# Two transposes moved from a DMA detour to VectorE, and a new way into the kernel: loads of x from ScalarE's queue, zero-tile passes ahead of the data, squares of x from a token-major load

## The chip, the cores and the metric

The kernel runs on one core of one Trainium2 chip. The metric is device time in microseconds, from the start to the end of one execution; the median of three runs is shown. Engines are named as in the profile: PE is TensorE's matmul side, PEld its weight load, DVE is VectorE, ACT is ScalarE, POOL is GpSimd, SP is SyncE, which issues most DMAs.

## What is computed

One residual block with two parallel token mixers, on 256 tokens of width 2048, all in float32:

```
h = RMSNorm(x);  p = h @ W_in
y_m = mlstm(p) @ W_up_m          # 4 heads, chunkwise, width 1024
y_s = s5(p) @ W_up_s             # 32 groups, 64 complex states each, width 512
merged = sigmoid(g_m) * y_m + sigmoid(g_s) * y_s
x = x + merged @ W_out
x = x + SwiGLU(RMSNorm(x))       # hidden width 5632
out = RMSNorm(x)
```

## The kernel before

**Blocks.** All weights are cut into blocks of 128 partitions x 1024 float32 (512 KB): two contraction tiles of 128 rows by 512 columns. The list `blocks` (L1139 to L1165) holds 427 of them in the order of use: `w_in`, the small head matrices, `w_glu`, `w_up_s` (8 blocks), `w_up_m` (16: four column quarters n of four blocks), `w_out` (32: four quarters of eight), the FFN's gate and up matrices and `w_ffn_down`. A float32 product is made of three passes: each operand is split into a rounded part hi and a rest lo, and hi\*hi, hi\*lo and lo\*hi are summed (`o2_block`, L160). `emit_dma` (L136) loads a block into a `raw` buffer from SP's queue, `emit_split` (L147) makes hi on ScalarE (L156) and lo = raw - hi on VectorE (L157). There are three `raw` and three hi/lo buffers; in the FFN every fourth block takes a `raw` from the ten larger `u8` buffers as soon as one is free.

**Order of the work.** The main loop (L1234) goes over the blocks. In iteration i it emits the load of block i+5, the split of block i+2, block i's passes with what follows them, and what earlier blocks left for later. `later(fn, delay)` (L1169) does that: work with delay 1 runs one iteration after the present one, with delay 0 at the end of the present list. `pump` (L208) places pieces of the S5 and mLSTM mixers between blocks during the first 140. A scheduler then orders each engine's instructions; `tc.issue_after` keeps an instruction behind another on its engine.

**The start.** x comes transposed (`xT`, feature-major) in five loads on SP's queue, between the first block loads (L1178, L1227, L1241). `xt_split` (L1184) scales it by the norm's gain and splits it into `hTh` and `hTl`. For the norm itself `xt_square` (L1197) squares the same tiles on ScalarE, pair by pair, and sums them on VectorE; `rms1` (L1206) sums over partitions with eight small passes on TensorE against a tile of ones and makes the reciprocal root `r1`, which is needed at the first evacuation of an accumulator. The first blocks are quarter 4 of `w_in`, whose passes are 256 columns wide (L853).

**The two transposes.** A product's result has tokens on the partitions; the next product needs features there. `upm_mm` (L951) forms a merged tile of 128 tokens x 512 features on VectorE after a quarter's last block and calls `turn` (L969). That transposes 32x32 squares inside their groups of 32 partitions (`blocks_T`, L273, one instruction of 128x512), and one iteration later moves the groups between the partitions by way of DRAM: `groups_dma` (L278) issues one write and four reads on GpSimd's queue. Two iterations after that the tile is split into `mTh` and `mTl`. `out_mm` (L988) adds the product to x after each quarter, and `x1_T` (L1008) does the same for the residual tiles: transposes, move, and a scale-and-split into `h2h` and `h2l`. There are eight merged and eight residual tiles. Contraction tiles 12 to 15 of `mTh`, the last merged quarter, are first read by block 6 of each quarter of `w_out`. The FFN uses `turn` too (22 tiles, L1068).

Of the kernel before, what the change touches and what calls it, by code (L numbers as in the profile page):

```python
# [17 lines left out]
P = 128  # L18
# [23 lines left out]
SQ = 3  # L42
GLU = 3
SLACK = 0.3


@with_exitstack
def block_kernel(ctx: ExitStack, tc: tile.TileContext, d, out):
# [18 lines left out]
    def u8(shape, dt=F32, name="u"):  # L67
        return up.tile(shape, dt, tag="u8", name=nm(name), bufs=NU8)
# [24 lines left out]
    def TT(o, a, b, op):  # L93
        return V.tensor_tensor(o, a, b, op=op)  # L94
# [7 lines left out]
    def f(ap):  # L102
        return ap.bitcast(F32)
# [5 lines left out]
    def pvs(n, i=None, w=1):  # L109
        a, b = PV[n]  # L110
        if i is None:
            return pv[:, a:b]
        return pv[:, a + i : a + i + w]
# [17 lines left out]
                blocks.append((d[name][n, kp], fn_maker, (n, kp)))  # L131

    raws, splits = {}, {}
    wdma = [None]

    def emit_dma(i):  # L136
        if i < len(blocks):
            if i == 3:
                raw = u32([P, 1024], name="raw")
            elif FFN0 + 4 <= i < len(blocks) - NTAIL - 4 and i % 4 == 3:  # L140
                raw = u8([P, 1024], name="raw")
            else:
                raw = wp.tile([P, 1024], F32, tag="raw", name=nm("raw"), bufs=NRAW)
            wdma[0] = nc.sync.dma_start(raw, blocks[i][0]).ins
            raws[i] = raw

    def emit_split(i):  # L147
        if i < len(blocks):
            raw = raws.pop(i)
            if i >= len(blocks) - NTAIL:  # L150
                hl = u8([P, 2, 1024], F32R, name="hl")
                hi, lo = hl[:, 0], hl[:, 1]
            else:
                hi = wp.tile([P, 1024], F32R, tag="hi", name=nm("hi"), bufs=NHI)
                lo = wp.tile([P, 1024], F32R, tag="lo", name=nm("lo"), bufs=NHI)
            A.copy(hi, raw)  # L156
            TT(lo, raw, f(hi), SUB)  # L157
            splits[i] = (hi, lo)

    def o2_block(acc, lhs, kts, hi, lo, first, last):  # L160
# [112 lines left out]
    def blocks_T(o, i):  # L273
        V.transpose(o.rearrange("p j a c -> p a j c"), i.rearrange("p (a j c) -> p a j c", a=4, j=4))  # L274
# [676 lines left out]
    def upm_mm(i, nk, hi, lo):  # L951
        n, kp = nk
        if n == 0 and kp == 0:
            mlg.until("out")
            cur["mTh"] = [u8([P, 8, 256], F32R, name="mTh") for _ in range(2)]
            cur["mTl"] = [u8([P, 8, 256], F32R, name="mTl") for _ in range(2)]
        oh, ol = ml["out"]
        if kp == 0:
            cur["acc"] = [acc_tile(), acc_tile()]
        o2_block(cur["acc"], lhs_of([oh], [ol], 8), (2 * kp, 2 * kp + 1), hi, lo, kp == 0, kp == 3)  # L960
        if kp == 3:
            for tt in range(2):
                o = gate_ap("gm", tt, n)
                TT(o, cur["acc"][tt], o, MUL)
                TT(o, o, gate_ap("gs", tt, n), ADD)
                v = lambda a: a[n // 2][:, n % 2 * 4 : n % 2 * 4 + 4, :]
                turn(n, tt, o, v(cur["mTh"]), v(cur["mTl"]))

    def turn(n, tt, src, th, tl):  # L969
        st_ = m2([P, 4, 4, 32])  # L970
# [35 lines left out]
            later(lambda: x1_T(n))  # L1006

    def x1_T(n):  # L1008
        sd = u8([P, 2, 1024], name="x1sd")
        st_ = sd[:, 0].rearrange("p (t j a c) -> p t j a c", j=4, t=2, a=4)  # L1010
        for tt in range(2):
            blocks_T(st_[:, tt], cur["x1"][:, tt, n * 512 : n * 512 + 512])

        def move():
            for tt in range(2):
                groups_dma(
                    sd[:, 1].rearrange("p (t i x) -> p t i x", t=2, i=4)[:, tt],
                    sd[:, 0].rearrange("p (t j x) -> p t j x", j=4, t=2)[:, tt],
                )
            later(split)  # L1020

        def split():
            d_ = sd[:, 1].rearrange("p (t i a c) -> p a (t i) c", i=4, t=2, a=4)
            for a in range(4):
                ct = 4 * n + a
                v = lambda h: h[ct // 8][:, ct % 8, :].rearrange("p (i c) -> p i c", c=32)
                A.activation(v(cur["h2h"]), d_[:, a], AF.Copy, scale=pvs("g2", ct))
                STT(v(cur["h2l"]), d_[:, a], pvs("g2", ct), f(v(cur["h2h"])), MUL, SUB)

        later(move, 0)  # L1030
        if n == 3:
            s = cp.tile([P, 2], F32, name="ssum2")
            V.tensor_reduce(s, ss2, mybir.AxisListType.X, ADD)
            TS(s, s, 1.0 / D, EPS, MUL, ADD)
            rstd(r2, s, "r2")
# [133 lines left out]
    def later(fn, delay=1):  # L1169
        laters.append([delay, fn])  # L1170
# [1 line left out]

    SL = NHI - 1
    DL = SL + NRAW
    xt = {}
    s1 = cp.tile([P, 2], F32, name="s1")

    def xt_dma(a, n):  # L1178
        t = (u16 if a >= 8 else u8)([P, n, 256], name="xt")
        nc.sync.dma_start(t.rearrange("p a b -> p (a b)"), d["xT"][:, a * 256 : (a + n) * 256])  # L1180
        for k in range(n):
            xt[a + k] = t[:, k, :]

    def xt_split(kp):  # L1184
        for kt in (2 * kp, 2 * kp + 1):
            oh_ = hTh[kt // 8][:, kt % 8, :]
            ol_ = hTl[kt // 8][:, kt % 8, :]
            g = pvs("gmix", kt)
            A.activation(oh_, xt[kt], AF.Copy, scale=g)
            STT(ol_, xt[kt], g, f(oh_), MUL, SUB)  # L1190

    one2 = cp.tile([P, 2], F32, name="one2")
    nc.gpsimd.memset(one2, 1.0)
    A.copy(cp.tile([P, 2], F32, name="warm"), one2)
    xq = u8([P, 3, 512], name="xq")

    def xt_square(kp):  # L1197
        a = xt[2 * kp]
        b = xt[2 * kp + 1]
        o = xq[:, 0 if kp == 0 else 1 + kp % 2]  # L1200
        A.activation(o[:, 0:256], a, AF.Square)
        A.activation(o[:, 256:512], b, AF.Square)
        if kp:
            TT(xq[:, 0], xq[:, 0], o, ADD)

    def rms1():  # L1206
        ps_ = aux()
        for tt in range(2):
            for h in range(2):
                c = h * 256 + tt * 128  # L1210
                mm(ps_[:, tt * 2 : tt * 2 + 2], xq[:, 0, c : c + 128], one2, h == 0, h == 1)
        TS(s1, ps_[:, 0:4].rearrange("p (a b) -> p a b", b=2)[:, :, 0], 1.0 / D, EPS, MUL, ADD)
# [12 lines left out]
    s5g = Gen(s5_gen())  # L1225
    mlg = Gen(ml_gen())
    for k in range(4):  # L1227
        xt_dma(*((0, 2), (2, 2), (4, 4), (8, 4))[k])
        emit_dma(k)
    for kp in range(2):  # L1230
        xt_split(kp)
        emit_split(kp)

    for i in range(len(blocks)):  # L1234
        if i == 0:
            for k in range(4, DL):
                emit_dma(k)
        emit_dma(i + DL)
        with tc.issue_after(wdma[0]):
            if i == 0:  # L1240
                xt_dma(12, 4)  # L1241
# [3 lines left out]
            if i == 4:  # L1245
                nc.sync.dma_start(cst, d["cst"])
                A.copy(identr, ident)
                A.copy(maskr, maskf)
            if i == 9:
                nc.sync.dma_start(wif, d["wif"])  # L1250
            if i == 6:
                s5["bT"] = u8([P, 4, 2, 128], name="s5bT")
                nc.sync.dma_start(s5["bT"], d["s5bT"])
        if i + SL < 8:
            xt_split(i + SL)
        emit_split(i + SL)
        if 0 <= i - SQ + 1 < 8:
            xt_square(i - SQ + 1)
        hi, lo = splits.pop(i)
        blocks[i][1](i, blocks[i][2], hi, lo)  # L1260
        run = [l for l in laters if l[0] <= 0]
        laters = [[l[0] - 1, l[1]] for l in laters if l[0] > 0]
        if i == 6 + SQ:
            rms1()
        for l in run:
            l[1]()
        fn, (n, kp) = blocks[i][1], blocks[i][2]
        t = 2.59 if fn in (win_mm, ups_mm, upm_mm) else 1.31
        if fn is win_mm and kp == 7 and n > 4:
# [85 lines left out]
```

## Time and profile before

| what | value |
|---|---|
| median of 3 runs | 1259.12 us (1258.21 to 1259.77) |
| the profiled execution's own time | 1258.85 us |
| its span in the profile | 1257.1 us |
| PE, PEld busy | 1233.7 us (98%), 1015.3 us |
| DVE, ACT, POOL busy | 803.8 us (64%), 604.0 us (48%), 106.6 us |
| mean granted clock of TensorE | 0.995 |
| DMA on GpSimd's queue (the detours) | 7904 packets, 19.94 MB |
| all DMA | 258.19 MB, mean 205 GB/s |

The span runs from the first to the last instruction; 1.75 us of the execution's own time lie around it. Passes on TensorE overlap: a pass of 512 columns is listed with 0.39 us while passes start some 0.23 us apart, so a busy PE is not a PE at its peak, and counts of passes in windows of equal length say more. The idle time of an engine off the chain costs nothing.

### The profile page before, as it was taken

The page shows a single profiled execution, that of the slowest core. Times are in us where ns is not written, and L with a number is a line of the kernel's source. Part 1 is how long each engine was busy: PE and PEld are TensorE (multiplying, and loading weights), DVE is VectorE, ACT ScalarE, POOL GpSimd, SP SyncE. Part 2 cuts the span into 40 slices and gives each one's busy share as a digit, 9 for nine tenths or more (in the row PEclk, how much of TensorE's full clock was granted, in tenths as well). Part 3 has the DMA queues.
Part 4 walks back from the last instruction along what each step waited for, and adds up shares of the span by engine and source line. Part 5 has one row for each costly group of instructions (what it writes and reads, how often), then busy time and mean ns, then how long its engine had stood idle before and what let it go on. Part 6 is the DMA issues. An engine that isn't in the chain of part 4 may idle for free.

```text
span 1257.1 us, 15683 instructions
## 1 busy us (share of the span) xinstructions
PE 1233.7 (98%) x5738; PEld 1015.3 (81%) x5738; DVE 803.8 (64%) x1162; ACT 604.0 (48%) x752; POOL 106.6 (8%) x199
## 2 busy tenths in 40 slices
PE   7999999999999999989999999999999999999997
PEld 7777888887788878868888888888888888888885
DVE  8779945999877856645556555555555554554544
ACT  7574554446654445444344444434444443444433
POOL 0000000000000522211101100110111010000000
PEclk9999999999999999989999999999999999999999
DMA  7645655554555977877667766555765686666443
GB/s 265 208 137 178 194 184 182 167 160 143 190 182 193 280 265 256 286 239 224 217 203 228 222 212 217 187 184 204 245 228 183 225 279 198 196 198 199 152 161 141
DMA packets 75597, 258.19 MB, mean 205 GB/s; under 512 B 10496, under 2 KB 11264, under 8 KB 75520
## 3 DMA queue, kind: packets, MB, share of 16 engines
q1 hardware_dynamic: 67616, 237.25, 58.1%
q0 software_dynamic: 7904, 19.94, 4.8%
q8 instruction: 45, 0.74, 0.2%
q14 instruction: 32, 0.26, 0.1%
HBM read 245.09 MB, written 12.06 MB: 205 GB/s over the span
## 4 chain that ended last, share of the span: by engine, by line
PE 85%; DVE 6%; DMA 5%; issue 2%; ACT 1%; ACTq 0%; SPq 0%; DVEq 0%
PE acc L100 80%; PE aux L100 4%; DMA raw<-in_w_out_dram 4%; DVE lo L94 3%; ACT hi L156 1%; DMA raw<-in_w_ffn_gate_dram 1%; DVE xcT L97 1%; DVE stm L94 0%; DVE bu L94 0%; DMA raw<-in_w_up_m_dram 0%; DVE x L94 0%; DVE gm L94 0%; DMA raw<-in_w_in_dram 0%; PE aux L774 0%; DVE h2l L97 0%
## 5 line engine op out<-in xcount | busy, mean ns | idle before, releaser
L94 DVE TENSOR_TENSOR lo<-raw,hi 128x1024 fp32r<-128x1024 f32 x427 | 521.0, 1221 | 403.6 <-ACT hi L156 403.0
L156 ACT CAST hi<-raw 128x1024 fp32r<-128x1024 f32 x427 | 449.1, 1053 | 577.5 <-PE acc L100 488.9
L100 PE MATMUL acc<-lo,h2h 128*128 128x512 f32 x704 | 275.2, 391 | 0.6 <-DVE lo L94 0.5
L100 PE MATMUL acc<-hi,h2l 128*128 128x512 f32 x704 | 274.2, 390 | 0.0
L100 PE MATMUL acc<-hi,h2h 128*128 128x512 f32 x704 | 246.8, 391 | 4.2 <-ACT hi L156 4.2
L100 PE MATMUL acc<-hi,aT 128*128 128x512 f32 x664 | 204.6, 389 | 0.0
L100 PEld LDWEIGHTS acc<-hi,h2h 128*128 128x128 f32 x704 | 132.5, 189 | 32.7 <-ACT hi L156 5.3
L100 PEld LDWEIGHTS acc<-lo,h2h 128*128 128x128 f32 x704 | 132.7, 189 | 29.6 <-DVE lo L94 2.1
L100 PE MATMUL acc<-lo,hTh 128*128 128x512 f32 x384 | 153.6, 400 | 1.3 <-DVE lo L94 1.2
L100 PEld LDWEIGHTS acc<-hi,h2l 128*128 128x128 f32 x704 | 132.8, 189 | 27.4
L100 PE MATMUL acc<-hi,hTl 128*128 128x512 f32 x384 | 150.4, 392 | 0.0
L100 PEld LDWEIGHTS acc<-hi,aT 128*128 128x128 f32 x664 | 124.7, 188 | 25.9
L100 PE MATMUL acc<-hi,hTh 128*128 128x512 f32 x384 | 139.4, 393 | 0.0
L100 PE MATMUL acc<-lo,aT 128*128 128x512 f32 x332 | 129.1, 389 | 0.0
L100 PEld LDWEIGHTS acc<-lo,hTh 128*128 128x128 f32 x384 | 72.1, 188 | 22.1 <-DVE lo L94 4.0
L100 PEld LDWEIGHTS acc<-hi,hTh 128*128 128x128 f32 x384 | 71.7, 188 | 16.7 <-issue 2.0
L100 PEld LDWEIGHTS acc<-hi,hTl 128*128 128x128 f32 x384 | 72.2, 188 | 14.6 <-issue 0.7
L281 POOL DMA_DIRECT2D bounce<-m x30 | 16.9, 565 | 690.5 <-DVE m L274 690.2
L100 PEld LDWEIGHTS acc<-lo,aT 128*128 128x128 f32 x332 | 62.3, 188 | 12.9
L283 POOL DMA_DIRECT2D m<-bounce x120 | 65.6, 554 | 43.1 <-DMA bounce<-m 28.2
L100 PE MATMUL acc<-lo,mTh 128*128 128x512 f32 x128 | 50.0, 392 | 0.0
L100 PE MATMUL acc<-hi,mTl 128*128 128x512 f32 x128 | 49.5, 389 | 0.0
(246 smaller groups left out, 1077.7 us busy)
## 6 DMA issues: line engine op xcount, KB each, us to landing
raw<-in_w_in_dram SPq DMA_DIRECT2D x104, 512.0 KB, 3.5
raw<-in_w_ffn_gate_dram SPq DMA_DIRECT2D x88, 512.0 KB, 3.7
raw<-in_w_ffn_up_dram SPq DMA_DIRECT2D x88, 512.0 KB, 4.2
raw<-in_w_ffn_down_dram SPq DMA_DIRECT2D x88, 512.0 KB, 3.5
raw<-in_w_out_dram SPq DMA_DIRECT2D x32, 512.0 KB, 5.0
raw<-in_w_up_m_dram SPq DMA_DIRECT2D x16, 512.0 KB, 3.6
bounce<-m POOLq DMA_DIRECT2D x30, 256.0 KB, 4.1
m<-bounce POOLq DMA_DIRECT2D x120, 64.0 KB, 4.2
```

Source lines behind the costliest of these rows:

```text
L94: return V.tensor_tensor(o, a, b, op=op)
L97: return V.scalar_tensor_tensor(out=o, in0=a, scalar=s, in1=b, op0=op0, op1=op1, **kw)
L100: return PE.matmul(o, l, r, start=start, stop=stop, skip_group_check=True)
L156: A.copy(hi, raw)
L281: nc.gpsimd.dma_start(bounce, st_)
L283: nc.gpsimd.dma_start(dt_[32 * j : 32 * j + 32], bounce.rearrange("(i r) j x -> r i j x", i=4)[:, :, j])
```

## The change

Merged tiles and residual tiles are no longer moved through DRAM. `blocks_across` transposes each 32x32 square straight to its place in another partition group: sixteen VectorE instructions a tile, each from 32 partitions to 32 partitions, four squares (128 columns) wide. The two tiles of a merged quarter are turned at the end of its last block's iteration and one iteration later, those of a residual quarter one and two iterations after its last block; the scale-and-split of the residual then comes in operations of 128 columns instead of 256. The FFN's `turn` stays. At the start, the first eight tiles of `xT` come in four loads on ScalarE's queue, with the activation table's first load behind them; block 0 is loaded, and split, in two halves; six passes on a zeroed tile, which feed nothing, are put ahead of TensorE's work. The squares are taken from a second load of x, token-major, 2 MB on SP's queue at blocks 3 and 4: four ScalarE operations of 1024 columns that sum as they go, emitted at block 8. The constants' load moves from block 4 to 5.

```diff
+NWARM = 6
...
+    def pieces(i):
+        return (slice(0, 512), slice(512, 1024)) if i == 0 else (slice(0, 1024),)
...
-            wdma[0] = nc.sync.dma_start(raw, blocks[i][0]).ins
+            for p_ in pieces(i):
+                wdma[0] = nc.sync.dma_start(raw[:, p_], blocks[i][0][:, p_]).ins
...
-            A.copy(hi, raw)
-            TT(lo, raw, f(hi), SUB)
+            for p_ in pieces(i):
+                last = A.copy(hi[:, p_], raw[:, p_]).ins
+                TT(lo[:, p_], raw[:, p_], f(hi[:, p_]), SUB)
+                if i == 0 and p_.start == 0:
+                    with tc.issue_after(last):
+                        xt_split_kt(1)
...
-                turn(n, tt, o, v(cur["mTh"]), v(cur["mTl"]))
+                later(lambda tt=tt, o=o, th=v(cur["mTh"]), tl=v(cur["mTl"]): turn_here(n, tt, o, th, tl), tt)
+
+    def blocks_across(o, i):
+
+        v = i.rearrange("p (a j c) -> p a j c", a=4, j=4)
+        for q in range(4):
+            for j in range(4):
+                V.transpose(o[32 * j : 32 * j + 32, :, 32 * q : 32 * q + 32], v[32 * q : 32 * q + 32, :, j])
+
+    def turn_here(n, tt, src, th, tl):
+        dt_ = m2([P, 4, 128])
+        blocks_across(dt_, src)
+        v = lambda a: a[:, :, tt * 128 : tt * 128 + 128]
+        A.copy(v(th), dt_)
+        TT(v(tl), dt_, f(v(th)), SUB)
...
     def x1_T(n):
...
+        d_ = u8([P, 4, 256], name="x1d")
+
+        def part(tt):
+            ts_ = slice(tt * 128, tt * 128 + 128)
+            blocks_across(d_[:, :, ts_], cur["x1"][:, tt, n * 512 : n * 512 + 512])
             for a in range(4):
                 ct = 4 * n + a
+                v = lambda h: h[ct // 8][:, ct % 8, ts_]
+                A.activation(v(cur["h2h"]), d_[:, a, ts_], AF.Copy, scale=pvs("g2", ct))
+                STT(v(cur["h2l"]), d_[:, a, ts_], pvs("g2", ct), f(v(cur["h2h"])), MUL, SUB)
+
+        part(0)
+        later(lambda: part(1), 0)
...
+    zw = m2([P, 256])
+    nc.gpsimd.memset(zw, 0.0)
+    zp = aux()
+    for k in range(NWARM):
+        mm(zp[:, 0:256], zw[:, 0:128], zw, True, True)
+    for a, n in ((0, 1), (1, 1), (2, 2), (4, 4)):
+        xt_dma(a, n, nc.scalar)
...
+    with tc.issue_after(adma[0]):
+        A.copy(cp.tile([P, 2], F32, name="warm"), one2)
+    ssx = cp.tile([P, 2, 2], F32, name="ssx")
+
+    def x_squares():
         for tt in range(2):
             for h in range(2):
+                v = xs[0][:, tt, h * 1024 : h * 1024 + 1024]
+                A.activation(v, v, AF.Square, accum_out=ssx[:, tt, h : h + 1])
...
     def rms1():
+        TT(s1, ssx[:, :, 0], ssx[:, :, 1], ADD)
+        TS(s1, s1, 1.0 / D, EPS, MUL, ADD)
         rstd(r1, s1, "r1")
...
-    for k in range(4):
-        xt_dma(*((0, 2), (2, 2), (4, 4), (8, 4))[k])
+    for k in range(3):
         emit_dma(k)
-    for kp in range(2):
-        xt_split(kp)
-        emit_split(kp)
+    xt_dma(8, 4, nc.sync)
+    emit_dma(3)
+    xt_split_kt(0)
+    emit_split(0)
+    xt_split(1)
+    emit_split(1)
...
+            if i == 3:
+                xs.append(u16([P, 2, 2048], name="xs"))
+            if i in (3, 4):
+                nc.sync.dma_start(xs[0][:, i - 3], d["x"][(i - 3) * 128 : (i - 2) * 128])
+            if i == 5:
                 nc.sync.dma_start(cst, d["cst"])
...
-        if 0 <= i - SQ + 1 < 8:
-            xt_square(i - SQ + 1)
+        if i == 8:
+            x_squares()
```

## Rows read from the trace of the kernel before

**Rows 1.** The chain of waits, its shares of the span by engine and line.

```profile
by line: PE acc L100 80.3%; PE aux L100 4.4%; DMA raw<-in_w_out_dram 3.5%; DVE lo L94 2.6%; issue 1.6%; ACT hi L156 1.2%; DMA raw<-in_w_ffn_gate_dram 1.2%; DVE xcT L97 0.7%; DVE stm L94 0.5%; DVE bu L94 0.4%; DMA raw<-in_w_up_m_dram 0.4%; D
```

**Rows 2.** Windows of 4 us: length, busy of PE, PEld, DVE, ACT, POOL, clock, DMA, GB/s.

```profile
20.00:24.00 4.00, 4.00 (x36) 4.00 (x35) 4.00 (x12) 2.75 (x7) 0.00 (x0) 1.00 0.60 160
448.00:452.00 4.00, 2.47 (x10) 1.57 (x10) 2.89 (x3) 1.57 (x2) 0.00 (x0) 1.00 0.79 276
532.00:536.00 4.00, 3.21 (x15) 2.32 (x13) 0.00 (x0) 0.00 (x0) 0.21 (x1) 1.00 1.02 398
536.00:540.00 4.00, 1.68 (x3) 0.96 (x4) 1.72 (x2) 2.62 (x3) 4.00 (x8) 0.72 0.89 337
540.00:544.00 4.00, 4.00 (x10) 2.72 (x9) 1.86 (x2) 0.42 (x1) 0.15 (x1) 0.50 0.83 262
544.00:548.00 4.00, 2.35 (x9) 1.51 (x9) 2.71 (x5) 2.65 (x5) 0.00 (x0) 0.93 0.63 194
552.00:556.00 4.00, 4.00 (x19) 3.32 (x18) 1.97 (x2) 3.84 (x5) 0.00 (x0) 1.00 0.55 157
```

**Rows 3.** Timeline of VectorE in w_up_m: start, us, instruction.

```profile
405.68 1.22 DVE L94 TENSOR_TENSOR lo<-raw,hi 128x1024 fp32r<-128x1024 f32 x1 [1.08 <-ACT hi L156]
408.39 1.22 DVE L94 TENSOR_TENSOR lo<-raw,hi 128x1024 fp32r<-128x1024 f32 x1 [1.50 <-ACT hi L156]
409.54 1.28 DVE L94 TENSOR_TENSOR gm<-acc,gm 128x512 f32<-128x512 f32 x2
410.74 1.28 DVE L94 TENSOR_TENSOR gm<-gm,gs 128x512 f32<-128x512 f32 x2
411.94 1.22 DVE L94 TENSOR_TENSOR lo<-raw,hi 128x1024 fp32r<-128x1024 f32 x1
413.07 1.29 DVE L274 STREAM_TRANSPOSE m<-gm 128x512 f32<-128x512 f32 x2
414.29 1.18 DVE L94 TENSOR_TENSOR lo<-raw,hi 128x1024 fp32r<-128x1024 f32 x1
...
419.09 0.68 DVE L94 TENSOR_TENSOR mTl<-m,mTh 128x512 fp32r<-128x512 f32 x1
```

**Rows 4.** Timeline at the first FFN blocks, idle time before and its releaser in brackets.

```profile
528.04 1.15 POOL L281 DMA_DIRECT2D bounce<-x1sd  x2 [11.13 <-DVE x1sd L274]
...
537.19 1.04 ACT L156 CAST hi<-raw 128x1024 fp32r<-128x1024 f32 x1 [7.16 <-DMA raw<-in_w_ffn_gate_dram]
...
538.28 1.22 PE L100 MATMUL acc<-hi,h2h 128*128 128x512 f32 x2 [3.07 <-ACT hi L156]
```

**Rows 5.** Windows: the second quarter of w_up_m, and 20 us of w_out.

```profile
409.54:420.83 11.29, 11.29 (x51) 9.34 (x51) 9.51 (x14) 5.26 (x6) 6.09 (x13) 1.00 0.86 268
480.00:500.00 20.00, 20.00 (x88) 16.26 (x87) 12.08 (x14) 9.74 (x15) 5.49 (x10) 1.00 0.84 278
```

**Rows 6.** Timeline of ScalarE and TensorE at the start.

```profile
4.49 0.91 ACT L1189 ACTIVATE hTh<-xt,pv 128x256 fp32r<-128x256 f32 x2 [2.27 <-DMA xt<-in_xT_dram]
...
6.84 0.58 PE L100 MATMUL acc<-hTh,hi 128*128 128x256 f32 x1 [6.84 <-ACT hi L156]
...
8.71 1.05 PE L100 MATMUL acc<-hTh,lo 128*128 128x256 f32 x4
...
13.07 0.64 PE L100 MATMUL acc<-hTh,lo 128*128 128x256 f32 x4
...
35.68 0.95 PE L100 MATMUL aux<-one,xq 128*128 128x2 f32 x8
```

**Rows 7.** Timeline of VectorE: short operations, and pairs of 256 columns.

```profile
35.29 0.47 DVE L94 TENSOR_TENSOR s5sm<-s5sm 128x16 f32<-128x16 f32 x4
...
42.29 0.85 DVE L94 TENSOR_TENSOR s5sp<-m,m 64x256 f32<-64x256 f32 x2
...
44.31 0.75 DVE L94 TENSOR_TENSOR m<-s5c,s5sm 128x256 f32<-128x256 f32 x2
```

**Rows 8.** Groups by form: an operation of 128x128, busy and mean ns.

```profile
L94 DVE TENSOR_TENSOR m<-s5sp 128x128 f32<-128x128 f32 x2 | 0.6, 292 | 0.1
```

More of the change, by code (lines that the diff above doesn't have):

```diff
@@ L1008, in x1_T @@
     def x1_T(n):
[L1009 to L1023, printed above, removed]
+        d_ = u8([P, 4, 256], name="x1d")
+        def part(tt):
+            ts_ = slice(tt * 128, tt * 128 + 128)
+            blocks_across(d_[:, :, ts_], cur["x1"][:, tt, n * 512 : n * 512 + 512])
             for a in range(4):
                 ct = 4 * n + a
[L1026 to L1030, printed above, removed]
+                v = lambda h: h[ct // 8][:, ct % 8, ts_]
[3 more added lines that the diff above has]
+        later(lambda: part(1), 0)
         if n == 3:
@@ L1174, in block_kernel, with xt_dma @@
     DL = SL + NRAW
-    xt = {}
+    xt, adma, xt16 = {}, [None], []
     s1 = cp.tile([P, 2], F32, name="s1")
-    def xt_dma(a, n):
-        t = (u16 if a >= 8 else u8)([P, n, 256], name="xt")
-        nc.sync.dma_start(t.rearrange("p a b -> p (a b)"), d["xT"][:, a * 256 : (a + n) * 256])
+    def xt_dma(a, n, eng):
+        if a < 8:
+            t = u8([P, n, 256], name="xt")
+        else:
+            if a == 8:
+                xt16.append(u16([P, 8, 256], name="xt"))
+            t = xt16[0][:, a - 8 : a - 8 + n, :]
+        adma[0] = eng.dma_start(t.rearrange("p a b -> p (a b)"), d["xT"][:, a * 256 : (a + n) * 256]).ins
@@ L1181, in xt_dma, with xt_split_kt @@
         for k in range(n):
             xt[a + k] = t[:, k, :]
+    def xt_split_kt(kt):
+        oh_ = hTh[kt // 8][:, kt % 8, :]
+        ol_ = hTl[kt // 8][:, kt % 8, :]
+        g = pvs("gmix", kt)
+        A.activation(oh_, xt[kt], AF.Copy, scale=g)
+        STT(ol_, xt[kt], g, f(oh_), MUL, SUB)
     def xt_split(kp):
         for kt in (2 * kp, 2 * kp + 1):
[L1186 to L1189, printed above, removed]
@@ L1190, in xt_split @@
-            STT(ol_, xt[kt], g, f(oh_), MUL, SUB)
+            xt_split_kt(kt)
+    zw = m2([P, 256])
[5 more added lines that the diff above has]
+        xt_dma(a, n, nc.scalar)
     one2 = cp.tile([P, 2], F32, name="one2")
     nc.gpsimd.memset(one2, 1.0)
[L1194 to L1204, printed above, removed]
@@ L1206, in rms1 @@
-    def rms1():
-        ps_ = aux()
+    with tc.issue_after(adma[0]):
+        A.copy(cp.tile([P, 2], F32, name="warm"), one2)
+    ssx = cp.tile([P, 2, 2], F32, name="ssx")
+    def x_squares():
         for tt in range(2):
             for h in range(2):
-                c = h * 256 + tt * 128
-                mm(ps_[:, tt * 2 : tt * 2 + 2], xq[:, 0, c : c + 128], one2, h == 0, h == 1)
-        TS(s1, ps_[:, 0:4].rearrange("p (a b) -> p a b", b=2)[:, :, 0], 1.0 / D, EPS, MUL, ADD)
+                v = xs[0][:, tt, h * 1024 : h * 1024 + 1024]
+                A.activation(v, v, AF.Square, accum_out=ssx[:, tt, h : h + 1])
@@ L1213, in rms1 @@
+    xs = []
+    def rms1():
+        TT(s1, ssx[:, :, 0], ssx[:, :, 1], ADD)
+        TS(s1, s1, 1.0 / D, EPS, MUL, ADD)
         rstd(r1, s1, "r1")
@@ L1240, in block_kernel @@
             if i == 0:
-                xt_dma(12, 4)
+                xt_dma(12, 4, nc.sync)
             if i == 7:
@@ L1244, in block_kernel @@
                 nc.sync.dma_start(s5["cc"], d["s5c"])
-            if i == 4:
+            if i == 3:
[3 more added lines that the diff above has]
+            if i == 5:
                 nc.sync.dma_start(cst, d["cst"])
```

## The prediction

> **What bounds it now.** I read the chain of waits first, then the windows, then single instructions. The chain is TensorE's accumulating passes for 80% of the span; loads of `w_out` blocks hold 3.5%, the casts and subtractions that split a block into hi and lo hold 3.8% together [rows 1]. So a change pays only where TensorE waits. The 4 us windows find those places by the count of passes: 19 is a full window, and five windows fall short: 10, 15, 3, 10 and 9 [rows 2]. That is 9+4+16+9+10 = 48 passes missing. A block is twelve passes and takes 2.71 us (two successive lo subtractions start at 405.68 and 408.39 [rows 3]), so 0.226 us a pass and **10.9 us** in all: 2.0 near 450, where the last merged quarter has come back from DRAM among `w_out` loads, and 8.9 at the first FFN blocks. There a cast waits 7.16 us for a `w_ffn_gate` block, TensorE stands 3.07 us [rows 4], and the granted clock falls to 0.72, 0.50 and 0.93 of 2.4 GHz in the next windows [rows 2]. Two bounces of the residual are issued 9 us before that cast [rows 4]. Everywhere else near the change TensorE is fed in time; the margin that matters there is VectorE's. In the second quarter of `w_up_m` it is busy 9.51 of 11.29 us [rows 5].
>
> **The start.** TensorE's first pass is at 6.84, behind the first cast [rows 6]. Its 24 passes of block 0 run 0.21 us apart (four in 1.05, the last itself 0.41) and later ones 0.12 apart (four in 0.64) [rows 6]: the engine had been idle, and it runs first at 1.2 and then at 2.4 GHz. If six zero passes have it at the higher level when data comes, 24 x 0.09 = 2.2 us are saved; if they raise nothing, none. A half block and a 128 KB first piece of x let the first cast start earlier and take half of its 1.04 us [rows 4], but the zero passes, fp32 and at the low clock, lie in front on TensorE: between no gain and 1.5 us, I take 0.5, nearer to none because of them. The eight small passes on `xq` go (0.95 us with the overlap of the last; 0.8 on the path [rows 6]). Sum **-3.5**, between -0.8 and -4.5. The four loads issued from ScalarE's queue, with the table load now behind them, lie in 2.27 us in which ScalarE waits for x [rows 6]; past that cover they would move the first cast by what is over, and this is in the range. Squares: sixteen short ScalarE operations and seven VectorE adds go, four of 1024 columns come (about a cast's 1.04 each); ScalarE had 2.75 of 4.00 us busy between 20 and 24 [rows 2], so both cost nothing. The 2 MB of token-major x ride on SP's queue behind the loads of blocks 8 and 9: 5 us at the 398 GB/s of the densest window [rows 2], at a time when 160 GB/s are moved [rows 2]. Weights queued behind wait up to 2.6 us each; their buffers are asked for about three blocks ahead, 8 us, so nothing. Cover gone, it would be 1 to 2 us at block 10.
>
> **What the DMA detour gives back.** Sixteen tiles lose a DRAM write, four reads and GpSimd's five issues each. Nothing then delays mT or h2 but VectorE, and the weight loads run alone. Kept: all of the 48 passes, **-10.9**. Bounds: far-ahead FFN blocks are also in that queue, so the FFN wait could stay except for the bounce's 0.5 MB (1.3 us at 398 GB/s): -3.3.
>
> **What VectorE gets instead.** One transpose of 128x512 per tile (two in 1.29, so 0.60 to the next [rows 3]) becomes sixteen of 32 partitions x 128 columns. No row has such an instruction. Below: 16-column operations follow each other every 0.10 us (four in 0.47 [rows 7]); sixteen would be 1.6. Middle: from 0.10 at 16 columns and 0.60 at 512, 0.215 at 128: 3.4. Above: a whole 128x128 operation, 0.29 [rows 8], with no overlap: 4.6. **I take 4.6**, for this reason: two 256-column operations on all partitions take 0.75, so the second starts 0.33 after the first; two of the same width whose outputs start at partition 0 and then 64 take 0.85, that is twice a full 0.42 [rows 7]. Overlap is lost when the starting partition moves, and in the new helper the output moves by 32 partitions with every instruction.
>
> The Trainium skill says so as a rule (VectorE: DVE Perf Modes, section Two Vector instructions with no wait between them): an instruction whose input or output starts in another group of 32 partitions than the one before is held until all earlier ones have finished. The pair above agrees with it; by it the sixteen cost 4.6, without it 3.4.
>
> **VectorE's balance around `w_up_m`.** Per quarter, four blocks and 10.8 us of TensorE: four lo at 1.13, 4.5; two multiplies and two adds, 2.4 (409.54 to 411.94); two mTl, 1.2; transposes 1.2 now, 9.3 after [rows 3]. That is 9.3 now and 17.4 after. It can't be put off: block 6 of `w_out`'s first quarter reads the last merged quarter. From the first merged quarter to that block there are 18 blocks, 48.8 us of TensorE, in which VectorE owes 17 lo (19.2), four quarters of multiply, add and mTl (14.4) and eight tiles (37.1): 70.7. TensorE comes **21.9 us** late, whatever the order. (At 3.4 a tile 12.3; at 1.6 nothing.) Behind the transposes on VectorE stand the lo, for which TensorE's second pass of each block waits. On ScalarE the mTh copies (and in `w_out` the h2h scales, now eight short ones for four) wait for the transposes instead of the bounce, with hi casts queued behind; such a cast is late no longer than the lo that stands behind the same transposes, so it adds nothing of its own.
>
> **VectorE's bursts in `w_out`.** Per quarter 21.7 us of TensorE, and VectorE owes eight lo (9.0), two adds (1.2), two tiles (9.3), eight h2l, now of 128 columns (2.3): 21.8, against some 12 busy in 20 now [rows 5]. The sum just fits, the order doesn't: behind a quarter's end come adds (to 1.2), a lo (2.3), a tile and its h2l (8.1), a lo (9.3), the second tile and h2l (15.0), and a lo at 16.2 which TensorE wants at 11.1. In this order 5.1 us are lost at each of four quarter ends (the last in FFN's first blocks), with the lo in front none. I take 3.5, nearer to the order of the issue: **+14** (0 to 20.4).
>
> **Sum.** -3.5 - 10.9 + 21.9 + 14 = +21.5, on the profiled execution's 1258.85 us: 1280.4, so **1280**; the median of the runs shown is 0.3 above that execution, which changes nothing. The likeliest case's own bounds: +21.9 - 15.4 = +6.5 with no bursts and the best start, to 21.9 + 20.4 - 0.8 - 3.3 = +38 with full bursts and the least return: 1265 to 1297.
>
> **Rivals.**
> *The transposes are cheap.* At 1.6 a tile VectorE owes 46.4 in the 48.8 us and 15.7 in `w_out`'s 21.7: it fits, and -14.4 remains: 1244. For it: a quarter of the partitions might stream faster, and 1.6 is what short operations cost. Against it: 512 columns take 0.60 and 16 take 0.10, a transpose no less than an add, so columns are paid one by one. It spans 1243 to 1252 by the bounds of the return. It decides the sign below about 3.2 us a tile, and below 1.9 nothing at all is lost. Chance 0.20; this is the one on the other side.
> *No hold.* At 3.4 a tile: 12.3 late before block 6; in `w_out` the same walk has its third lo at 13 or so against 11.1, 2 us or none, I take 1: +4. -14.4 + 16.3 = +2: 1261, from 1254 to 1270. For it: operations on the same partitions do overlap. Against it: the 64-partition pair. Chance 0.22, of which 0.07 faster, 0.07 within the bound.
> *The clock falls too.* TensorE stood 3.07 us and then ran at 1.2 GHz [rows 2, 4]; a 1.5 us stop near 450 left 1.00. Two tiles in one go hold lo back by 5 us; each such stop adds some 16 passes at 0.2 more, 3.3 us, at four to eight places less what VectorE gains meanwhile: about +13, 1293. Chance 0.13.
> *The start doesn't start.* Zero passes that last longer than the loads, or raise no clock, move every case by up to 3.5; no sign of the forecast changes.
>
> **Numbers.** The forecast has 0.45. What a measurement of this kernel can tell from no change is about 0.2%, 2.5 us. Faster: the cheap case 0.20 and 0.07 of the no-hold case, 0.27. Within: 0.07 and 0.03 of the forecast's lower end, 0.10. Slower: 0.63. The range leaves out the cheapest outcomes and the longest stops, some 0.1 each: 1248 to 1296.
>
> **What would show it.** The mean of a 32x128 transpose and the time sixteen take: 4.6 right, 3.4 no hold, under 2 the cheap case. VectorE full between about 400 and 450, TensorE's waits there put down to lo instead of `w_out` loads. Full windows at the first FFN blocks but for stops behind x1's transposes. Passes 0.12 apart from the first, near 6. Wrong: VectorE with idle time around `w_up_m`, or a lo that overtakes the transposes so that no wait is longer than 2 us.

## The result and the profile after

The changed kernel takes 1299.16 us (median of 4 runs, 1297.75 to 1301.53) and the kernel before 1259.44 (4 runs, 1258.21 to 1259.89): 1.0317 times as long, 95% interval 1.0301 to 1.0332. The forecast was 1280, from 1248 to 1296: the sign was right, the size was 39.7 us where 21.3 were forecast, and the range ends 3 us short. The profiled execution took 1297.75 us, its span is 1296.0 and its mean granted clock 0.987.

The chain of waits is read first, as [rows 1] were:

```profile
by line: PE acc L101 78.7%; PE aux L101 4.2%; DVE lo L95 3.2%; DVE m L984 2.7%; DVE x1d L984 2.7%; issue 1.9%; DMA xt<-in_xT_dram 0.7%; DVE gm L95 0.7%; ACT hi L163 0.6%; DVE x L95 0.4%; DVE xcT L98 0.4%; DVE bu L95 0.4%; PE aux L784 0.3%; 
```

The loads of `w_out` and `w_ffn_gate`, 4.7% together in [rows 1], are no longer among its first entries; x's own load has come in, with 0.7% or 9.7 us, all of it at the start. The new transposes of both helpers (line 984) hold 5.4%, about 70 us of the end's path. So the exchange that was forecast took place, at a higher price. Where it was paid shows on VectorE (start, length, instruction; the rows answer to [rows 3], with the first add of `w_out` behind):

```profile
398.51 1.28 DVE L95 TENSOR_TENSOR gm<-acc,gm 128x512 f32<-128x512 f32 x2
...
402.05 10.13 DVE L984 STREAM_TRANSPOSE m<-gm 32x128 f32<-32x128 f32 x32
412.20 0.69 DVE L95 TENSOR_TENSOR mTl<-m,mTh 128x512 fp32r<-128x512 f32 x1
412.81 3.49 DVE L95 TENSOR_TENSOR lo<-raw,hi 128x1024 fp32r<-128x1024 f32 x3
...
458.00 10.13 DVE L984 STREAM_TRANSPOSE m<-gm 32x128 f32<-32x128 f32 x32
...
468.77 3.49 DVE L95 TENSOR_TENSOR lo<-raw,hi 128x1024 fp32r<-128x1024 f32 x3
472.17 0.69 DVE L95 TENSOR_TENSOR mTl<-m,mTh 128x512 fp32r<-128x512 f32 x1
...
484.58 1.28 DVE L95 TENSOR_TENSOR x<-acc,x 128x512 f32<-128x512 f32 x2
```

Thirty-two transposes, two tiles, take 10.13 us: 0.317 each, 5.06 a tile, where 4.6 had been taken. From 398.51 to the last mTl's end at 472.86 VectorE is busy but for 0.6 us in which it waits for an accumulator. Twice whole pairs of tiles stand in front of three lo. TensorE pays for it (timeline of TensorE; in brackets its idle time before and what ended it; the first five rows answer to [rows 6]):

```profile
1.10 5.12 PE L101 MATMUL aux<-m 128*128 128x256 f32 x12 [1.10 <-POOL one L1223]
5.94 0.51 PE L101 MATMUL acc<-hTh,hi 128*128 128x256 f32 x2
...
7.42 0.63 PE L101 MATMUL acc<-hTh,lo 128*128 128x256 f32 x4
8.42 0.51 PE L101 MATMUL acc<-hTh,hi 128*128 128x256 f32 x2 [0.36 <-ACT hi L163]
...
11.15 0.39 PE L101 MATMUL acc<-hTh,hi 128*128 128x256 f32 x1 [1.04 <-ACT hi L163]
...
414.08 0.79 PE L101 MATMUL acc<-lo,oh 128*128 128x512 f32 x1 [6.05 <-DVE lo L95]
...
434.56 0.50 PE L101 MATMUL acc<-lo,oh 128*128 128x512 f32 x1 [2.77 <-DVE lo L95]
...
452.86 0.80 PE L101 MATMUL acc<-lo,mTh 128*128 128x512 f32 x1 [5.52 <-DVE lo L95]
...
470.04 0.79 PE L101 MATMUL acc<-lo,mTh 128*128 128x512 f32 x1 [7.15 <-DVE lo L95]
...
479.44 0.62 PE L101 MATMUL acc<-hi,mTh 128*128 128x512 f32 x2
...
572.21 0.50 PE L101 MATMUL acc<-lo,h2h 128*128 128x512 f32 x1 [1.56 <-DVE lo L95]
...
578.24 0.50 PE L101 MATMUL acc<-lo,h2h 128*128 128x512 f32 x1 [2.99 <-DVE lo L95]
```

Each of these stops from 414 on ends with a lo of VectorE (one of 0.68 us at 424.91, not shown, ends with a cast). The stop before 470.04 stands in the fourth block of `w_out`'s first quarter; at 479.44 its block 6, the first reader of the last merged quarter, begins. The windows (columns as in [rows 2]) show what the long stops do to the granted clock; the first three lie in the first `w_out` quarter, the next three at the first FFN blocks, and the last answers to the second of [rows 5]:

```profile
448.00:452.00 4.00, 0.00 (x0) 0.00 (x0) 3.85 (x12) 1.09 (x2) 0.00 (x0) 0.68 0.00 0
464.00:468.00 4.00, 0.00 (x0) 0.00 (x0) 3.82 (x14) 0.64 (x1) 0.00 (x0) 0.81 0.00 0
468.00:472.00 4.00, 1.96 (x5) 1.58 (x6) 3.97 (x5) 0.62 (x1) 0.00 (x0) 0.50 0.16 53
...
572.00:576.00 4.00, 3.04 (x12) 2.17 (x12) 3.75 (x14) 0.09 (x1) 0.00 (x0) 1.00 0.71 260
576.00:580.00 4.00, 1.76 (x6) 1.44 (x7) 4.00 (x11) 3.97 (x8) 0.00 (x0) 0.89 0.12 42
580.00:584.00 4.00, 4.00 (x13) 3.17 (x13) 2.52 (x5) 1.62 (x2) 0.00 (x0) 0.68 0.92 311
480.00:500.00 20.00, 16.93 (x74) 13.38 (x73) 17.21 (x41) 9.98 (x19) 0.00 (x0) 1.00 0.46 157
```

TensorE does nothing while VectorE is full, and the clock is at 0.50 afterwards. In `w_out`, 74 passes stand where 88 stood.

The marks below, the start of one and the same instruction on VectorE in three kernels, say how much was lost where. "Whole" is the changed kernel with one 128x512 transpose in the place of sixteen, told of below; it has no detour through DRAM and no price on VectorE.

| mark, us | before | whole | changed | changed less whole |
|---|---|---|---|---|
| first multiply of the merged branch | 398.66 | 399.09 | 398.51 | -0.6 |
| first add at the end of `w_out`'s quarter 1 | 456.28 | 453.49 | 484.58 | +31.1 |
| quarter 2 | 479.70 | 475.25 | 510.15 | +34.9 |
| quarter 3 | 501.13 | 497.01 | 536.12 | +39.1 |
| quarter 4 | 523.91 | 518.77 | 561.58 | +42.8 |
| product after the first `w_ffn_up` quarter | 573.18 | 562.35 | 611.90 | +49.6 |
| end of the span | 1257.1 | 1246.4 | 1296.0 | +49.6 |

So 31.7 us are lost between the first merged quarter and the first `w_out` quarter's end, 3.8, 4.2 and 3.7 in the next three and 6.7 at the first FFN blocks; nothing behind them, and nothing is won ahead of them.

### The profile page after: what moved, and what is told of

It is laid out like the page before. It is cut to its first block, busy times and chain, and to the rows that moved or that the text cites. A ratio compares the mean times of both kernels' runs of the same rounds, so it can differ in the third digit from the quotient of the medians.

```text
span 1296.0 us, 15771 instructions
## 1 busy us (share of the span) xinstructions
PE 1244.9 (96%) x5742; PEld 1020.5 (79%) x5742; DVE 870.6 (67%) x1413; ACT 607.6 (47%) x761; POOL 62.8 (5%) x120
## 3 DMA queue, kind: packets, MB, share of 16 engines
q10 hardware_dynamic: 576, 1.05, 0.2%
## 4 chain that ended last, share of the span: by engine, by line
PE 83%; DVE 12%; issue 2%; DMA 1%; ACT 1%; ACTq 0%; DVEq 0%
PE acc L101 79%; PE aux L101 4%; DVE lo L95 3%; DVE m L984 3%; DVE x1d L984 3%; DMA xt<-in_xT_dram 1%; DVE gm L95 1%; ACT hi L163 1%; DVE x L95 0%; DVE xcT L98 0%; DVE bu L95 0%; PE aux L784 0%; DMA raw<-in_w_ffn_gate_dram 0%; DMA raw<-in_w_out_dram 0%; DVE stm L95 0%
## 5 line engine op out<-in xcount | busy, mean ns | idle before, releaser
L95 DVE TENSOR_TENSOR lo<-raw,hi 128x1024 fp32r<-128x1024 f32 (+1 forms) x428 | 521.4, 1220 | 374.1 <-ACT hi L163 373.1
L163 ACT CAST hi<-raw 128x1024 fp32r<-128x1024 f32 (+1 forms) x428 | 449.4, 1051 | 586.2 <-PE acc L101 508.8
L101 PEld LDWEIGHTS acc<-lo,hTh 128*128 128x128 f32 x384 | 72.1, 188 | 21.9 <-DVE lo L95 4.5
L291 POOL DMA_DIRECT2D bounce<-m x22 | 12.4, 566 | 867.9 <-DVE m L284 867.9
L101 PEld LDWEIGHTS acc<-lo,mTh 128*128 128x128 f32 x128 | 25.0, 195 | 31.1 <-DVE lo L95 26.0
```

The source lines that it names most:

```text
L101: return PE.matmul(o, l, r, start=start, stop=stop, skip_group_check=True)
L163: last = A.copy(hi[:, p_], raw[:, p_]).ins
L291: nc.gpsimd.dma_start(bounce, st_)
```

## The experiments

My theory after this reading: all of the loss is VectorE's, because each transpose waits for the end of the one before; the balance of the forecast counted only sums and not the order; the start brings next to nothing. The rivals are that the start or its 2 MB load cost something, that a transpose of 32 partitions takes its 0.3 us wherever it lies, and that the granted clock made the loss.

### The parts of the change

**The new start alone.** The two helpers are those of before, so tiles and residual go through DRAM again.

```
-                later(lambda tt=tt, o=o, th=..., tl=...: turn_here(n, tt, o, th, tl), tt)
+                turn(n, tt, o, v(cur["mTh"]), v(cur["mTl"]))
...
(and x1_T as before)
```

> The new start alone: first loads of x on ScalarE's queue, half blocks, zero passes, squares from the token-major load. Both transposes keep the detour through DRAM. My theory after reading the changed kernel: worth nothing, 1259 us within 1.5, because the first real pass comes 0.9 us earlier and the third block's weights then make TensorE wait again; the first multiply of the merged branch comes at 398.5, as in the changed kernel. Rival, the term as forecast: 3.5 less, 1255.5, with the first multiply near 395.

It measured 1262.75 (12 runs, 1260.03 to 1267.32) against 1259.37 (17 runs): 1.0025, from 1.0008 to 1.0041. Both values of mine missed: it is 3.4 us slower. The execution that was profiled is the slowest of the twelve (1267.32), so its marks show more than the medians do. In it the first multiply of the merged branch is at 398.09, 0.6 earlier than before, so the start itself loses nothing; the loss stands where the last merged quarter comes back from DRAM (timeline of ScalarE):

```profile
452.01 1.04 ACT L163 CAST hi<-raw 128x1024 fp32r<-128x1024 f32 x1 [4.33 <-DMA raw<-in_w_out_dram]
```

TensorE's stop here is 5.2 us, where the kernel before had 1.5. The first add of `w_out` comes at 461.73, against 456.28. In this execution the loss belongs to the detour that the change removes. Whether the new start brings it about, or the two profiled executions only differ, wasn't tried.

**The transposes alone**, with the old start (the two helpers of the change, put into the kernel before).

> The transposes on VectorE alone, with the old start. My theory: all of the loss is here, 1299 us within 2. Rival: the new start hides part of it or adds to it by the 2 MB of token-major x, then 1302 or 1296.

1300.02 (5 runs, 1298.74 to 1301.21; ratio 1.0320, from 1.0299 to 1.0341). All of the loss is here. With the new start on top the median is 0.9 us less, which is inside the spread of either kernel.

**One tile kind at a time**, with the new start: only the merged branch turned on VectorE, then only the residual.

> The changed kernel with only the merged branch turned on VectorE; the residual goes through DRAM as before. Theory from the marks of the runs (first add of w_out 31.1 us later than with whole transposes; the detour's part from there to the end 8.2): 1248.3 + 31.1 + 8.2 = 1287.6 within 3. Rival (the forecast's 21.9 and all of the detour's 8.9): 1279.

> The changed kernel with only the residual turned on VectorE; the merged branch goes through DRAM as before. Theory from the marks (the four quarters' bursts 18.4 us, the detour's part up to the first add of w_out 2.8): 1248.3 + 18.4 + 2.8 = 1269.5 within 3. Rival (14 us of bursts, as forecast): 1265.

1288.95 (ratio 1.0230, from 1.0206 to 1.0253) and 1273.40 (1.0105, from 1.0083 to 1.0126). The first is as added up from the marks. The second is 3.9 over, outside what I had allowed. In it TensorE stops 4.3 us for a `w_out` block near 450, and the first add of `w_out` comes at 461.39: the same place as with the start alone. So the terms of `w_up_m` and of `w_out` do add; what doesn't add is the detour.

### What a transpose costs

**No move between partitions, one instruction per tile.**

```
-        for q in range(4):
-            for j in range(4):
-                V.transpose(o[32 * j : 32 * j + 32, :, 32 * q : 32 * q + 32], v[32 * q : 32 * q + 32, :, j])
+        V.transpose(o.rearrange("p a (j c) -> p a j c", j=4), v)
```

> The changed kernel with one 128x512 transpose per tile in the place of sixteen; it leaves out the move between groups of partitions. VectorE then has what it had before, and no detour through DRAM is left. This measures what the DMA detour gives back by itself. Theory: the 10.9 us of TensorE's missing passes return, the start gives nothing: 1248 us, full windows at the first FFN blocks. Rival: the FFN's first loads are late without the bounces too, only 3.3 us return: 1256.

1248.34 (4 runs, 1248.20 to 1248.69): 0.9910, from 0.9891 to 0.9930. The forecast's reading of the detour was right. At the first FFN blocks, where [rows 2] had 15, 3, 10 and 9 passes, the windows are full:

```profile
536.00:540.00 4.00, 4.00 (x20) 3.30 (x19) 2.45 (x3) 2.32 (x3) 0.00 (x0) 1.00 0.76 275
540.00:544.00 4.00, 4.00 (x19) 3.34 (x18) 2.80 (x4) 3.23 (x5) 0.00 (x0) 1.00 0.74 257
```

TensorE has no stop in this kernel between 396 and 640, so I take it as the floor for any way of turning the tiles; the changed one lies 50.8 us above it.

**Sixteen transposes that stay on their partitions.**

```
-                V.transpose(o[32 * j : 32 * j + 32, :, 32 * q : 32 * q + 32], v[32 * q : 32 * q + 32, :, j])
+                V.transpose(o[32 * q : 32 * q + 32, :, 32 * j : 32 * j + 32], v[32 * q : 32 * q + 32, :, j])
```

> The changed kernel with each 32x128 transpose writing to the 32 partitions that it reads, so four in a row stay on one group and three of four starts change no partition. It leaves out the move of blocks between the groups of partitions. Theory (an instruction whose partitions start elsewhere than the one before waits for its end): inside a group of four 0.215 to 0.23 us apart, 0.317 at the fourth, so about 4.0 us a tile for 5.06, VectorE's 16 tiles 17 us shorter, and with VectorE the bound the kernel 12 to 17 us faster than the changed one, about 1285. Rival (a transpose of 32 partitions takes its 0.30 whatever its place, no overlap is there to lose): 0.317 throughout and 1299.

1274.35 (4 runs; 1.0119, from 1.0099 to 1.0140), 24.8 us faster than the changed kernel, more than the 12 to 17 that I had expected. The group and the first pair of tiles, by form and in the timeline:

```profile
L984 DVE STREAM_TRANSPOSE m<-gm 32x128 f32<-32x128 f32 x128 | 28.4, 271 | 0.5
```

```profile
401.44 7.18 DVE L984 STREAM_TRANSPOSE m<-gm 32x128 f32<-32x128 f32 x32
```

Same shape, same count, same reads: 7.18 us for thirty-two in the place of 10.13. The single starts in the trace (medians over all 256) show how: on one group of partitions the four start 0.24, 0.19 and 0.19 us apart, each some 0.07 before the end of the one before; the step to the next group takes 0.27, and that transpose starts 0.01 after the end of the one before. In the changed kernel all of them start 0.01 after that end. So the 0.215 that I had bounded is about the mean of the three (0.21), and the 0.317 is the length of one transpose, 0.30, and that 0.01. Sixteen tiles are 23.6 us shorter on VectorE, and the kernel is 24.8 shorter: what VectorE is given there comes out in the time nearly one for one.

**The output held, the input moving:**

```
-        for q in range(4):
-            for j in range(4):
+        for j in range(4):
+            for q in range(4):
```

> The changed kernel with the two loops of the new helper changed over: four transposes in a row write the same 32 partitions, and what they read moves by 32 partitions each time. The result is the same. With the output moving and the input held for four, thirty-two took 10.13 us; with both held for four 7.18 us. Theory (a move of either end makes an instruction wait): 0.317 throughout, thirty-two in 10.1 us, 1299 us within 2. Rival (only a move of the output counts): thirty-two in about 7.2 us and 1274 us, as with both held.

1298.77 (4 runs, 1297.34 to 1299.50), the changed kernel's time, and its pace:

```profile
402.20 10.12 DVE L984 STREAM_TRANSPOSE m<-gm 32x128 f32<-32x128 f32 x32
```

So a move of the input alone is enough to lose the overlap, and neither order of the two loops saves anything: inside one tile no two transposes have both ends in the same groups. The Trainium skill states this (VectorE: DVE Perf Modes, section Two Vector instructions with no wait between them): an instruction is held until the earlier ones are finished when an input or its output starts in another group of 32 partitions than the last. These three runs agree, and put the price at 0.317 us for a held transpose behind another held one and at 0.19 to 0.24 for one that isn't held. An order over both tiles of a pair, in which each transpose is followed by the other tile's with the same two groups, wasn't tried.

### Order and clock

**Handed out in fours** over the following blocks, so that fewer stand ahead of a lo:

```
-    def blocks_across(o, i):
+    def blocks_across(o, i, qs=range(4)):
...
-        for q in range(4):
+        for q in qs:
...
-        blocks_across(dt_, src)
...
+        for q in range(4):
+            later(lambda q=q: blocks_across(dt_, src, (q,)), 2 * tt + q // 2)
...
+        later(split, 2 * tt + 1)
```

> The changed kernel with the merged branch's transposes handed out in fours over the next blocks, so that a lo stands behind some sixteen of them and not behind thirty-two. VectorE's work is the same. Theory (what the forecast's balance left out is the order: with the last thirty-two ahead of the lo of the fourth w_out block, TensorE still had five blocks of that quarter to do when VectorE was through): VectorE is through with the merged branch at about the same 473, TensorE is then two blocks further, no stop is over 4 us and the granted clock stays at 1.00 behind most of them; the first add of w_out comes 5 us earlier than 484.6, the whole 1294 us within 2. Rival (the order doesn't matter, VectorE's sum decides): 1299.

1291.79 (4 runs, 1290.83 to 1295.60), 7.4 us faster than the changed kernel with the same work, a little more than the 3 to 7 that I had expected. TensorE's stops (timeline) are more and shorter, and VectorE's last mTl ends at 477.04, 4.2 later than in the changed kernel, without harm. The adds at the end of `w_out`'s first quarter can't be compared: one comes at 476.95, the other at 485.02, where the changed kernel has both at 484.58. By count of passes TensorE is 6.4 us ahead there (its 97th pass on merged tiles starts at 478.46, in the changed kernel at 484.87), and the first add of quarter 2 comes at 504.43, 5.7 earlier:

```profile
428.20 0.50 PE L101 MATMUL acc<-lo,oh 128*128 128x512 f32 x1 [2.60 <-DVE lo L95]
...
448.29 0.79 PE L101 MATMUL acc<-lo,mTh 128*128 128x512 f32 x1 [3.37 <-DVE lo L95]
...
459.02 0.80 PE L101 MATMUL acc<-lo,mTh 128*128 128x512 f32 x1 [2.85 <-DVE lo L95]
```

The sum on VectorE had set only the earliest time at which the last merged tile can be there. In the changed kernel TensorE at that time, 472.86, stood in the fourth block of the quarter, because that block's lo was behind the same transposes, and block 6 began only at 479.44. The clock did not stay up, against what I expected: it is 0.58 and 0.50 in the windows behind the last two of these stops.

**Idle passes in the four long stops**, to keep TensorE at work:

```
+                if fill and q == 0 and tt == 0:
+                    fp = aux()
+                    for _ in range(fill):
+                        mm(fp, identr, h, True, True)
```

> The changed kernel with idle passes (20, 8, 18 and 24 of 512 columns, 0.227 us each) on TensorE in the four long stops of w_up_m and the start of w_out, between the first hi pass and the first lo pass of the waiting block; they write a tile that nobody reads. They take 4.5, 1.8, 4.1 and 5.4 us of stops of 6.05, 2.77, 5.52 and 7.15. Theory (VectorE is the bound up to the last of these stops): the granted clock stays at 1.00 behind them, but only the last stop's slow passes are won back, 1.4 us, so 1297.5 within 1.5. Rival (the clock's fall costs time at each of the stops, 32 passes of 0.2 us): 6.4 us faster, 1293.

1297.33 (4 runs, 1296.81 to 1297.77), 1.8 us faster by the medians. The clock (windows of this run) holds through the first and the last stop, where it had been 0.50:

```profile
412.00:416.00 4.00, 2.61 (x12) 1.84 (x11) 3.97 (x5) 0.62 (x1) 0.00 (x0) 1.00 0.18 37
...
452.00:456.00 4.00, 4.00 (x12) 3.17 (x11) 3.64 (x6) 0.78 (x1) 0.00 (x0) 0.57 0.86 260
...
468.00:472.00 4.00, 3.21 (x14) 2.31 (x14) 3.97 (x5) 0.62 (x1) 0.00 (x0) 1.00 0.17 31
```

The first add of `w_out` moves from 484.58 to 483.15, the 1.4 us of the last stop's slow passes. At the first stop the clock that holds brings 0.1 us: the first pass of `w_out` starts at 444.38, in the changed kernel at 444.46. At the second and third stops it fell all the same, where I had expected 1.00, so what it costs there isn't measured by this; that it costs nothing is argued from VectorE, which has no idle time up to 472.86 but the 0.6 us. So in `w_up_m` the fallen clock is a companion of the loss, not its cause: VectorE sets the time. At the first FFN blocks it wasn't tried.

### Another way to turn

**TensorE turns the tiles**, four 128x128 transposes each into a free accumulator bank, from which hi and lo are taken:

```
+    def turn_pe(src, th, tl):
+        ps_ = aux()
+        for a in range(4):
+            PE.transpose(ps_[:, a * 128 : a * 128 + 128], src[:, a * 128 : a * 128 + 128], ident)
+        o = ps_.rearrange("p (a c) -> p a c", a=4)
+        A.copy(th, o)
+        TT(tl, o, f(th), SUB)
...
(x1_T likewise, with the scale of g2)
```

> The changed kernel with all sixteen tiles turned by TensorE, four transposes of 128x128 each into a free accumulator bank; hi and lo are read from that bank. No DMA, no transposes on VectorE. The kernel's other transposes by TensorE follow each other 0.16 us apart, so a tile takes 0.65 us and sixteen 10.5 us of TensorE. Theory: 1248.3 (the run with whole transposes) plus 10.5: 1259, the same as the kernel before. Rival (the passes fill places where TensorE would wait, or VectorE's and ScalarE's saved work lets it run fuller): under 1256. Other rival (TensorE waits at each for the adds on VectorE): over 1262.

1254.92 (6 runs, 1254.34 to 1255.34): 0.9960 of the kernel before, from 0.9945 to 0.9974, so it beats both. Eight transposes start 0.108 us apart, not 0.16 (the kernel's other transposes by TensorE are 0.109 apart as well; I had misread them). From the first of the eight to the second pass behind them are 1.11 us, of which one pass is 0.23, so a tile costs 0.44 where VectorE took 5.06 (timeline, then a window at the first FFN blocks):

```profile
404.88 1.03 PE L982 MATMUL aux<-cst,gm 128*128 128x128 f32 x8
405.67 0.48 PE L101 MATMUL acc<-lo,oh 128*128 128x512 f32 x1
405.99 0.40 PE L101 MATMUL acc<-hi,ol 128*128 128x512 f32 x1
```

```profile
540.00:544.00 4.00, 4.00 (x19) 3.30 (x19) 1.58 (x2) 1.95 (x2) 0.00 (x0) 1.00 0.62 165
```

Sixteen are 7.0 us of TensorE; the kernel lies 6.6 above the floor of 1248.34, and TensorE waits for nothing between 396 and 640. So it is under 1256 because a transpose costs less than I had taken, and not because the passes fill idle places, as the rival has it: there are none to fill.

**The start, weighed in this kernel**, whose runs lie closer together: once with the old start, once with the new one without zero passes.

> The kernel with all sixteen tiles turned by TensorE (1254.9), but with the start of the kernel before. With no detour through DRAM its runs lie within 1 us of each other, so the start can be weighed more finely than with the detour. Theory (the new start brings 0.5 to 0.9 us, as the first stage marks of the runs so far show): 1255.6 within 0.7. Rivals: the forecast's 3.5, then 1258.4; the loss of 3.4 that the new start had together with the detour, then 1251.5.

> The same kernel with the new start and no zero passes ahead of the data. Theory: the first 24 to 36 passes come 0.21 us apart again in the place of 0.12, but the third block's weights, not the passes, set the pace up to 11 us, so the time is 1254.9 to 1255.9. Rival (the granted clock's early rise is worth the 2.2 us of the forecast): 1257.1.

1255.78 (10 runs, 1255.47 to 1257.27; ratio 0.9964, from 0.9951 to 0.9977) and 1254.07 (6 runs, 1253.77 to 1254.40; 0.9952, from 0.9934 to 0.9969). The new start brings 0.9 us by the medians, as it does between the transposes alone and the changed kernel. But in both pairs 0.4 us of that lie outside the span that the profile shows (in the two kernels with the old start 2.2 us of the execution's time lie around the span, in the two with the new 1.8); the spans themselves are 0.5 us shorter. Why the 0.4 differ stays open. Without zero passes, and with 2.2 us around the span again, it brings 1.7; 1254.07 is 0.8 below my range, and this is the fastest kernel measured that leaves nothing out. That the zero passes do harm isn't shown by this: the two kernels that differ in them alone were timed in different sets, on different chips, and their ratios overlap; the same holds for the 0.9. But they bring nothing, and the timeline of TensorE, with two rows of ScalarE behind it, shows why they aren't missed:

```profile
5.55 0.80 PE L101 MATMUL acc<-hTh,hi 128*128 128x256 f32 x2 [5.55 <-ACT hi L163]
...
8.07 1.05 PE L101 MATMUL acc<-hTh,lo 128*128 128x256 f32 x4
...
11.13 0.34 PE L101 MATMUL acc<-hTh,hi 128*128 128x256 f32 x1
...
9.17 0.91 ACT L1205 ACTIVATE hTh<-xt,pv 128x256 fp32r<-128x256 f32 x2 [1.12 <-DMA xt<-in_xT_dram]
9.99 1.04 ACT L163 CAST hi<-raw 128x1024 fp32r<-128x1024 f32 x1
```

The first pass comes at 5.55, where with zero passes in front it is 5.92 to 5.94; the first blocks run at the lower level; and the third block begins at 11.13 without a wait, where the changed kernel had been faster and then stood until 11.15. What decides is the third block's cast, and so the loads. I had taken it to wait for its weights. Here and in the changed kernel it stands behind two scalings of x that wait for x's load, until 9.17 and 9.25; with TensorE's turns and zero passes it does wait for the weights, until 10.39.

## Why the prediction was wrong

The terms of the sum against what the runs give for each:

| term, us | forecast | measured | from |
|---|---|---|---|
| start | -3.5 | -0.9 | TensorE turning, new start less old (-0.5 in the span) |
| detour | -10.9 | -10.1 | whole transposes, -11.0, less the start |
| `w_up_m` | +21.9 | +31.7 | marks, changed less whole |
| bursts | +14 | +18.4 | marks |
| sum | +21.5 | +39.1 | the kernel: +39.7 |

The mechanism was the one forecast: the transposes are held, VectorE becomes the bound, the detour's time comes back. Three terms were mis-sized, all to the same side.

**The balance of `w_up_m`**, 9.8 us, is the step that failed: "TensorE comes 21.9 us late, whatever the order". What the runs show in its place is 31.7. It has two parts. Each transpose was priced too low: 128 at 0.317 and not 0.29 are 3.5 us more, and VectorE's stretch measured 74.35 us for the 70.7 of the balance. The other 6.3 are the order: when VectorE was through at 472.86, TensorE needed 6.6 us more until block 6 began at 479.44. A sum of one engine's work bounds the time from below: it holds if TensorE has nothing left to do ahead of the last tile's reader. Here the pair of tiles was issued ahead of the lo of three blocks that come before that reader, so TensorE had them still to do, and 1.4 us of that come from passes at the low clock. Handing out the same work in fours took 7.4 us off the whole.

**The start.** The clock did rise early, as forecast: the four lo passes of the first half block at 7.42 take 0.63 us where [rows 6] have 1.05, and the first pass is 0.9 earlier than in [rows 6]. But 2.2 us of faster passes were put on the path without asking what is late next. The cast of the third block is, which ends TensorE's wait at 11.15, and more behind it. The chain of waits, which in the kernel before stands on TensorE from the first pass on (last row), now reaches TensorE only at 19.22:

```profile
2.13 9.66 DMA xt<-in_xT_dram
11.81 1.71 ACT hTh L1208 x4
13.52 0.95 ACT hi L163
...
17.97 1.21 DVE lo L95
19.22 24.61 PE acc L101 x160
...
6.84 29.00 PE acc L100 x206
```

Its head is the last of the four loads of x on ScalarE's queue, and behind that stand the splits of x and of the weights on ScalarE and VectorE. In all eleven profiled kernels with the new start it reaches TensorE at 18.3 to 19.8, with a load of weights at its head in seven and of x in four. So up to some 19 us TensorE's pace doesn't set the time there, with zero passes or without. That the squares and the 2 MB cost nothing fits the runs, but no run tries them alone.

**The bursts**, 4.4 us. 3.5 for each quarter end was close at three of them (3.8, 4.2, 3.7). The fourth is 6.7: there the stops are 1.56 and 2.99 us and the clock falls to 0.68. What part of it is the clock's, and whether another order would save these terms as it did in `w_up_m`, wasn't tried.

**The detour** was right to 0.8 us, and so was "held": of the three prices for a tile the dearest was chosen, for the reason that the runs confirm.

The rivals: with 0.60 a tile on VectorE the kernel takes 1248.3, near the 1244 of the cheap case, which had the start's 3.5 in it too. The case without the hold was 1261 at 3.4 a tile; at a measured 3.59 the kernel takes 1274, slower than before as well, since that price left out the order just the same. The clock's fall was seen at five places; of the 13 us that I gave it, 1.8 came back when idle passes were put into four of them, in two of which it fell all the same.

## What to carry to other kernels

A sum of work on an engine tells when it can be through, not when the work that others wait for is done: write down what is queued ahead of each operand, block by block, and count the blocks that are left. When an engine is at its limit for some 70 us, a 0.03 us error in the price of a small instruction that runs 128 times is worth the 3.5 us that a whole new start was forecast to bring. A tile of 128x512 that has to cross partitions cost 5.06 us on VectorE, more than eleven times the 0.44 that TensorE needed for it in this kernel's stream of passes, although TensorE is the engine that bounds it.

## What was not expected of the hardware

The kernels differ much in how far their runs spread: 1256.24 to 1265.09 in 17 runs of the kernel before and 1260.03 to 1267.32 in 12 with the new start, but 1248.20 to 1248.69 in 4, 1254.34 to 1255.34 in 6, 1255.47 to 1257.27 in 10 and 1253.77 to 1254.40 in 6 where no tile of these sixteen goes through DRAM and TensorE has no stop. That the detour makes the spread isn't shown: the kernel with the merged branch alone going through DRAM has 1272.33 to 1273.54, and the changed kernel, without the detour, 1297.75 to 1301.53, in 4 runs each.

The granted clock did not fall at once. After the stop of 2.77 us four passes started 0.23 us apart; from 435.84 on they were 0.42 apart:

```profile
434.90 0.39 PE L101 MATMUL acc<-hi,ol 128*128 128x512 f32 x1
...
435.84 0.63 PE L101 MATMUL acc<-lo,oh 128*128 128x512 f32 x1
436.26 0.63 PE L101 MATMUL acc<-hi,ol 128*128 128x512 f32 x1
```

The stop of 2.60 us in the kernel that hands its transposes out in fours left 1.00 in the windows around it.
